# One run instead of two for the small products at the start of the recurrence

## The chip, the cores and the metric

One core of one Trainium2 chip runs the whole program. The metric is device time in microseconds of one execution, taken as the median over several; the time before is 921.15 us (three runs, 920.98 to 921.52). The engines are named as the profile names them: PE does matrix products (PEld its weight loads), DVE, ACT and POOL do elementwise work, SP issues transfers.

## The reference, cut to what matters

Two layers. In each, a normalised input of 512 tokens by 1024 features is projected, and the projection feeds two branches: 16 heads of sliding-window attention, and 8 heads of a gated linear recurrence. The gated outputs are projected back, normalised and added. The recurrence is what the change touches:

```
def step(state, xs):                       # one chunk, all heads
    qch, kch, vch, b = xs                  # b: running sum of log forget gates
    decay = where(causal, exp(b_t - b_s), 0)
    scores = einsum('bhtd,bhsd,bhtsd->bhts', qch, kch, decay)
    o = einsum('bhts,bhsv->bhtv', scores, vch)
    o = o + einsum('bhtd,bhdv->bhtv', qch * exp(b), state)
    state = exp(b_last) * state + einsum('bhsd,bhsv->bhdv', kch * exp(b_last - b), vch)
```

## The kernel before, in words

Projections are done in `step()` (line 293): one step issues three products of 128x512, because every float32 operand is split in a high and a low half (`whi`, `wlo` for weights, made by ACT line 181 and DVE line 182; `hhi`, `hlo`, `ops` for the other operand). A *unit* is one output tile of a projection; it gathers in one of three PSUM banks named `pj`, and an evacuation on ACT or DVE (lines 851, 865, 889, 893) frees the bank. Up to two units run in turns.

The recurrence is worked out per head from small to large blocks. For each head, `prepare` makes `kb` and `qb`; `spread` (line 694) forms the base blocks of two tokens as 16 products of 32x32 outputs; `keep_spread` (line 698) copies the wanted elements on DVE into the head's score tile `a`. Then `hgrn(a)` works on four heads at once and runs six levels, hh = 2, 4, 8, 16, 32, 64: products of `k` and `q` (line 750 for the first four levels, 756 and 761 for the last two) into PSUM banks `sc`, a scaling of `q` on DVE (768) and of `k` on POOL (769) that the next level's products need, and a masked copy of the products into `a` (778, or ACT lines 783 and 788). After that the states and outputs follow (lines 796 to 831). For heads 0, 1 and 4, 5 the base blocks are made at the end of `prepare`; for heads 2, 3 and 6, 7 they are made at the head of `hgrn`, into banks `ac`. The change is there.

What sets the order is `merge`: it takes turns between the recurrence generator and the stream of projection steps. Each `yield w` in the recurrence says how many units of its own total it has used, and the stream with the smaller share used goes next. The total of a recurrence pass is `HG_N` plus what `prepare` yields. So the sum of all yields in `hgrn` and `HG_N` belong together:

```
merge((chain(prepare(2), hgrn(0), prepare(4)), HG_N + 14), rest(("in", l, FQ + 3)))
merge((chain(prepare(6), hgrn(4)), HG_N + 7), rest(("out", l, "h0")))
```

PE products are pinned in program order. DVE, ACT and POOL instructions are placed by a scheduler, each engine then works its list strictly in order. hgrn(0) runs beside projections whose banks ACT frees; hgrn(4) runs beside output projections too, whose banks DVE frees at line 893.

Of the kernel before, what the change touches and what calls it, by code (L numbers as in the profile page):

```python
# [32 lines left out]

W_BUFS = 9
RAW_BUFS = 4
HG_N = 53.5
VLAG = 4
QWAIT = 8
ROT_WAIT = 8
# [31 lines left out]
def hybrid_kernel(ctx: ExitStack, tc: tile.TileContext, x, wkv, win, wout, g_pre, g_post, lbp, ghead, sinks,  # L71
# [26 lines left out]
    def ac():  # L98
        ac_turn[0] += 1
        return ac_tiles[ac_turn[0] % len(ac_tiles)]  # L100
# [30 lines left out]
    for l in range(1, DEPTH):  # L131
        i = plan_order.index((l, "kv"))
# [310 lines left out]
    def layer(l, last):  # L443
# [253 lines left out]
        def keep_spread(j, bank):  # L697
            nc.vector.copy_predicated(As[j].rearrange("p (n t) -> p n t", n=NT), bmask.unsqueeze(1).broadcast_to([P, NT, P]),
                                      bank.rearrange("p (n t) -> p n t", n=NT))
# [31 lines left out]
        def hgrn(a):  # L731
            hs = [(j, *quad.pop(a + j)) for j in range(4)]
            banks = [ac(), ac()]
            for i in range(2):
                spread(a + 2 + i, banks[i])
            for i in range(2):
                keep_spread(a + 2 + i, banks[i])
            yield 1.5
            for hh in (2, 4, 8, 16, 32, 64):
                nb = SEQ // (2 * hh)  # L740
                per, qu = nb // NT, nb // NT // 4
                Ls = [sc(), sc()]
                for j, f, k, q in hs:
                    L, i = Ls[j // 2], j % 2
                    qv = q.rearrange("p (b two j) -> p b two j", two=2, j=hh)
                    if hh <= 16:
                        for n in range(NT):
                            for b in range(4):
                                o_, blk, c = n * P + 32 * b, n * per + b * qu, 256 * i + n * 64 + 16 * b
                                pin(nc.tensor.matmul(L[32 * b:32 * b + 32, c:c + 16], lhsT=k[:, o_:o_ + 32],  # L750
                                                     rhs=qv[:, blk:blk + qu, 1, :], start=True, stop=True, tile_position=(0, 32 * b)))
                    elif hh == 32:
                        for n in range(NT):
                            for b in range(2):
                                o_, r_, c = n * P + 64 * b, 64 * b + 32 * (n % 2), 64 * i + n // 2 * 32
                                pin(nc.tensor.matmul(L[r_:r_ + 32, c:c + 32], lhsT=k[:, o_:o_ + 32],  # L756
                                                     rhs=q[:, o_ + 32:o_ + 64], start=True, stop=True, tile_position=(0, r_)))
                    else:
                        for n in range(NT):
                            o_, b, c = n * P, n % 2, 128 * i + n // 2 * 64  # L760
                            pin(nc.tensor.matmul(L[64 * b:64 * b + 64, c:c + 64], lhsT=k[:, o_:o_ + 64],
                                                 rhs=q[:, o_ + 64:o_ + 128], start=True, stop=True))
                for two in (hs[:2], hs[2:]):
                    for j, f, k, q in two:
                        qv = q.rearrange("p (b two j) -> p b two j", two=2, j=hh)
                        kv_ = k.rearrange("p (b two j) -> p b two j", two=2, j=hh)
                        tv = tots[a + j].rearrange("p (b two) -> p b two", two=2)
                        nc.vector.tensor_tensor(qv[:, :, 1, :], qv[:, :, 1, :], tv[:, :, 0].unsqueeze(2).broadcast_to([P, nb, hh]), op=ALU.mult)  # L768
                        nc.gpsimd.tensor_tensor(kv_[:, :, 0, :], kv_[:, :, 0, :], tv[:, :, 1].unsqueeze(2).broadcast_to([P, nb, hh]), op=ALU.mult)  # L769
                        t2 = sm.tile([P, nb], F32, tag=f"tot{hh}", name=f"tot{hh}", bufs=4)  # L770
                        nc.vector.tensor_tensor(t2, tv[:, :, 0], tv[:, :, 1], op=ALU.mult)
                        tots[a + j] = t2
                    for j, f, k, q in two:
                        A, L, i = As[a + j], Ls[j // 2], j % 2
                        if hh <= 16:
                            Av = A.rearrange("p (n b two j) -> p n b two j", n=NT, two=2, j=hh)[:, :, :, 1, :]
                            mv = lmask[hh].rearrange("p (b j) -> p b j", j=hh).unsqueeze(1).broadcast_to([P, NT, per, hh])
                            nc.vector.copy_predicated(Av, mv, L[:, 256 * i:256 * i + 256].rearrange("p (n b j) -> p n b j", n=NT, j=hh))
                        elif hh == 32:
                            Av = A.rearrange("p (m two t) -> p m two t", m=NT // 2, two=2)  # L780
                            for b in range(2):
                                for e in range(2):
                                    nc.scalar.copy(Av[64 * b:64 * b + 32, :, e, 64 * b + 32:64 * b + 64],
                                                   L[64 * b + 32 * e:64 * b + 32 * e + 32, 64 * i:64 * i + 64].rearrange("p (m t) -> p m t", m=NT // 2))
                        else:
                            Av = A.rearrange("p (m b t) -> p m b t", m=NT // 2, b=2)
                            for b in range(2):
                                nc.scalar.copy(Av[0:64, :, b, 64:128],
                                               L[64 * b:64 * b + 64, 128 * i:128 * i + 128].rearrange("p (m t) -> p m t", m=NT // 2))
                    yield 3.0  # L790

            kps = []
            for j, f, k, q in hs:
                KP = sc()
                for n in range(NT - 1):
                    pin(nc.tensor.transpose(KP[:, n * P:(n + 1) * P], k[:, n * P:(n + 1) * P], ident))  # L796
                kst_ = tmp("u") if j == 0 else tmp("s")
                nc.scalar.copy(kst_[:, 0:384], KP[:, 0:384])
                kps.append(kst_)
                if j % 2:  # L800
                    yield 1.0
            vs = lambda j, n: vt[a // 4, n][:, j * P:(j + 1) * P]
            sts = {}

            def states(j):
                SU = ac()
                for n in range(NT - 1):
                    pin(nc.tensor.matmul(SU[:, n * P:(n + 1) * P], lhsT=kps[j][:, n * P:(n + 1) * P], rhs=vs(j, n), start=True, stop=True))  # L808
                st = sm.tile([P, 3, P], F32, tag="st", name="st", bufs=2)
                nc.scalar.copy(st[:, 0], SU[:, 0:P])  # L810
                for n in range(1, NT - 1):
                    nc.vector.scalar_tensor_tensor(st[:, n], st[:, n - 1], tots[a + j][:, n:n + 1], SU[:, n * P:(n + 1) * P],
                                                   op0=ALU.mult, op1=ALU.add)
                sts[j] = st

            def outputs(j):
                q, A = hs[j][3], As[a + j]
                O = ac()
                for n in range(NT):
                    c = slice(n * P, (n + 1) * P)  # L820
                    pin(nc.tensor.matmul(O[:, c], lhsT=A[:, c], rhs=vs(j, n), start=(n == 0), stop=False))  # L821
                for n in range(1, NT):
                    c = slice(n * P, (n + 1) * P)
                    pin(nc.tensor.matmul(O[:, c], lhsT=q[:, c], rhs=sts[j][:, n - 1], start=False, stop=(n == NT - 1)))  # L824
                Ov = O.rearrange("p (n t) -> p n t", n=NT)
                sq = tmp("s")
                nc.scalar.activation(sq, O, AF.Square)
                ss = sm.tile([P, 4], F32, tag="hss", name="hss")
                nc.vector.tensor_reduce(ss, sq.rearrange("p (n t) -> p n t", n=NT), axis=AX.X, op=ALU.add)
                r = rstd_of(ss, 4, P, "hr")  # L830
                nc.vector.tensor_tensor(q.rearrange("p (n t) -> p n t", n=NT), Ov, r.unsqueeze(2).broadcast_to([P, NT, P]), op=ALU.mult)
                on[a + j] = q

            for fn, j, w in ((states, 0, 1.5), (states, 1, 1.5), (outputs, 0, 2.0), (states, 2, 1.5), (outputs, 1, 2.0),
                             (states, 3, 1.5), (outputs, 2, 2.0), (outputs, 3, 2.0)):
                fn(j)
                yield w
# [342 lines left out]
```

## Time and profile before

| | |
|---|---|
| median of the runs | 921.15 us (920.98 to 921.52) |
| profiled execution, its own time | 922.98 us |
| its span, first to last instruction | 921.3 us |
| mean granted TensorE clock | 0.998 |
| PE busy | 904.2 us, 98% of the span |
| DVE, ACT, POOL busy | 667.0, 463.8, 273.9 us |
| HBM traffic | 108 GB/s over the span |

The span is the first to the last instruction on the core; 1.68 us of the execution's own time lie around it. A busy PE is read with care, since products overlap: a product of 128x512 is booked with 0.39 us, but they start 0.227 us apart. So starts are compared here, not durations. Rows of the timeline have the start, the time from the first start to the last end, the engine, the line, what is written from what, the shape and the count.

### The profile page before, as it was taken

The page shows a single profiled execution, that of the slowest core. Times are in us where ns is not written, and L with a number is a line of the kernel's source. Part 1 is how long each engine was busy: PE and PEld are TensorE (multiplying, and loading weights), DVE is VectorE, ACT ScalarE, POOL GpSimd, SP SyncE. Part 2 cuts the span into 40 slices and gives each one's busy share as a digit, 9 for nine tenths or more (in the row PEclk, how much of TensorE's full clock was granted, in tenths as well). Part 3 has the DMA queues.
Part 4 walks back from the last instruction along what each step waited for, and adds up shares of the span by engine and source line. Part 5 has one row for each costly group of instructions (what it writes and reads, how often), then busy time and mean ns, then how long its engine had stood idle before and what let it go on. Part 6 is the DMA issues. An engine that isn't in the chain of part 4 may idle for free.

```text
span 921.3 us, 19004 instructions
## 1 busy us (share of the span) xinstructions
PE 904.2 (98%) x7240; PEld 752.5 (82%) x7240; DVE 667.0 (72%) x1326; ACT 463.8 (50%) x1100; POOL 273.9 (30%) x292
## 2 busy tenths in 40 slices
PE   8999999999999999999999999999999999999996
PEld 6888887888888888888888878888888888888885
DVE  4977878859854797655786689776889449866556
ACT  5535757653664423534563466686446463245242
POOL 3424444303413042121332254451144022330102
PEclk9999999999999999999999999999999999999999
DMA  7594613322222332333355656122322323213413
GB/s 224 153 259 130 172 43 92 92 81 85 91 69 70 107 103 82 92 95 119 131 168 167 168 141 179 57 70 92 94 70 81 99 73 94 82 47 93 137 35 137
DMA packets 56570, 100.74 MB, mean 109 GB/s; under 512 B 6560, under 2 KB 9120, under 8 KB 56480
## 3 DMA queue, kind: packets, MB, share of 16 engines
q1 hardware_dynamic: 56192, 99.40, 36.4%
q8 instruction: 57, 0.93, 0.4%
q14 instruction: 33, 0.27, 0.1%
q10 hardware_dynamic: 288, 0.14, 0.1%
HBM read 86.93 MB, written 12.58 MB: 108 GB/s over the span
## 4 chain that ended last, share of the span: by engine, by line
PE 89%; DVE 6%; ACT 2%; issue 1%; POOL 1%; DMA 0%; POOLq 0%; DVEq 0%; ACTq 0%
PE pj L293 73%; PE sc L567 2%; PE ac L620 2%; PE sc L750 2%; PE ac L821 2%; DVE wlo L182 1%; PE ac L824 1%; PE ac L808 1%; PE sc L594 1%; ACT s L581 1%; PE sc L873 1%; PE sc L406 1%; PE sc L796 1%; DVE a L954 0%; PE sc L556 0%
## 5 line engine op out<-in xcount | busy, mean ns | idle before, releaser
L182 DVE TENSOR_TENSOR wlo<-raw,whi 128x512 fp32r<-128x512 f32 x249 | 182.8, 748 | 49.5 <-ACT whi L181 48.8
L181 ACT CAST whi<-raw 128x512 fp32r<-128x512 f32 x256 | 154.1, 620 | 105.9 <-PE pj L293 95.1
L293 PE MATMUL pj<-hhi,wlo 128*128 128x512 f32 x512 | 203.8, 398 | 0.0
L293 PE MATMUL pj<-hhi,whi 128*128 128x512 f32 x512 | 199.8, 390 | 0.0
L293 PE MATMUL pj<-hlo,whi 128*128 128x512 f32 x512 | 199.5, 390 | 0.0
L293 PE MATMUL pj<-whi,ops 128*128 128x512 f32 (+1 forms) x520 | 172.5, 394 | 0.0
L293 PEld LDWEIGHTS pj<-whi,ops 128*128 128x128 f32 x520 | 97.3, 188 | 19.3
L293 PEld LDWEIGHTS pj<-hhi,whi 128*128 128x128 f32 x512 | 96.1, 188 | 20.7
L293 PEld LDWEIGHTS pj<-hhi,wlo 128*128 128x128 f32 x512 | 96.2, 188 | 19.3
L293 PEld LDWEIGHTS pj<-hlo,whi 128*128 128x128 f32 x512 | 96.2, 188 | 18.6
L293 PE MATMUL pj<-whi,hlo 128*128 128x512 f32 x256 | 103.6, 405 | 0.0
L293 PE MATMUL pj<-wlo,ops 128*128 128x512 f32 (+1 forms) x260 | 100.8, 388 | 0.0
L293 PE MATMUL pj<-wlo,hhi 128*128 128x512 f32 x256 | 100.4, 392 | 0.3 <-DVE wlo L182 0.2
L293 PE MATMUL pj<-whi,hhi 128*128 128x512 f32 x256 | 100.3, 392 | 0.0
L769 POOL TENSOR_TENSOR k<-k,tot 128x256 f32<-128x256 f32 x80 | 64.6, 835 | 106.0 <-PE sc L750 56.5
L581 ACT ACTIVATE s<-sc,negm 128x128 f32<-128x128 f32 x128 | 45.5, 368 | 38.5 <-DVE negm L575 38.5
L768 DVE TENSOR_TENSOR q<-q,tot 128x256 f32<-128x256 f32 x80 | 48.3, 641 | 12.8 <-PE sc L756 7.0
L293 PEld LDWEIGHTS pj<-whi,hhi 128*128 128x128 f32 x256 | 48.1, 188 | 10.3
L293 PEld LDWEIGHTS pj<-wlo,ops 128*128 128x128 f32 x260 | 49.0, 188 | 8.8
L293 PEld LDWEIGHTS pj<-wlo,hhi 128*128 128x128 f32 x256 | 48.3, 189 | 8.8 <-DVE wlo L182 1.0
L293 PEld LDWEIGHTS pj<-whi,hlo 128*128 128x128 f32 x256 | 48.2, 188 | 8.1
L588 POOL TENSOR_TENSOR s<-s,sums 128x512 f32<-128x512 f32 x32 | 34.1, 1066 | 44.2 <-DVE sums L586 29.2
(188 smaller groups left out, 1418.1 us busy)
## 6 DMA issues: line engine op xcount, KB each, us to landing
raw<-in_win_dram SPq DMA_DIRECT2D x192, 256.0 KB, 2.7
raw<-in_wout_dram SPq DMA_DIRECT2D x64, 256.0 KB, 2.7
stack<-rot SPq DMA_DIRECT2D x16, 512.0 KB, 3.4
qs<-stack SPq DMA_DIRECT2D x32, 256.0 KB, 4.7
a<-in_x_dram SPq DMA_DIRECT2D x12, 256.0 KB, 3.7
raw<-in_wkv_dram SPq DMA_DIRECT2D x8, 256.0 KB, 4.1
x_mid<-a SPq DMA_DIRECT2D x8, 256.0 KB, 2.6
a<-x_mid SPq DMA_DIRECT2D x8, 256.0 KB, 3.2
```

The costliest lines, as they stand in the source:

```text
L181: keep(nc.scalar.copy(hi, v))
L182: keep((nc.gpsimd if i in on_pool and i % 2 else nc.vector).tensor_tensor(lo, v, hi.bitcast(F32), op=ALU.subtract))
L293: nc.tensor.matmul(u.o, lhsT=u.sta(k, u.w)[i], rhs=u.mov(k, u.w)[j], start=(n == 0), stop=(n == len(u.list) - 1))
L406: pin(nc.tensor.transpose(o[:, j * P:(j + 1) * P], self.xn[:, c, j * P:(j + 1) * P], ident))
L567: pin(nc.tensor.matmul(S[:, h * 256:(h + 1) * 256], lhsT=q[:, 2 * hp_ + h, t_], rhs=kst[v][p][:, (n - 1) * P:(n + 1) * P], start=(h == 0 a ...
L581: nc.scalar.activation(pt[:, h * P:(h + 1) * P], cur[h], AF.Exp, bias=negm[:, h:h + 1], scale=SCALE, accum_out=sums[:, h:h + 1])
L588: nc.gpsimd.tensor_tensor(pv, pv, sums.unsqueeze(2).broadcast_to([P, 4, P]), op=ALU.mult)
L620: pin(nc.tensor.matmul(U, lhsT=vst[v][:, blk, :], rhs=d, start=(i == 0), stop=(i == len(terms) - 1)))
L750: pin(nc.tensor.matmul(L[32 * b:32 * b + 32, c:c + 16], lhsT=k[:, o_:o_ + 32], rhs=qv[:, blk:blk + qu, 1, :], start=True, stop=True, tile_ ...
L768: nc.vector.tensor_tensor(qv[:, :, 1, :], qv[:, :, 1, :], tv[:, :, 0].unsqueeze(2).broadcast_to([P, nb, hh]), op=ALU.mult)
L769: nc.gpsimd.tensor_tensor(kv_[:, :, 0, :], kv_[:, :, 0, :], tv[:, :, 1].unsqueeze(2).broadcast_to([P, nb, hh]), op=ALU.mult)
L821: pin(nc.tensor.matmul(O[:, c], lhsT=A[:, c], rhs=vs(j, n), start=(n == 0), stop=False))
```

## The change

At the head of `hgrn`, the base blocks of the third and fourth head move from before the first pause to behind it, so that on PE they stand straight ahead of the products of level hh = 2. The pause is now 3.5 units and stands ahead of both (it was 1.5 and stood between them). The copies `keep_spread` are now issued behind the products of that first level. `HG_N` grows by the same two units.

```diff
-HG_N = 53.5
+HG_N = 55.5
...
         def hgrn(a):
             hs = [(j, *quad.pop(a + j)) for j in range(4)]
             banks = [ac(), ac()]
+            yield 3.5
             for i in range(2):
                 spread(a + 2 + i, banks[i])
-            for i in range(2):
-                keep_spread(a + 2 + i, banks[i])
-            yield 1.5
             for hh in (2, 4, 8, 16, 32, 64):
...
+                for i in range(2 if hh == 2 else 0):
+                    keep_spread(a + 2 + i, banks[i])
                 for two in (hs[:2], hs[2:]):
```

PE in hgrn(0) of the first layer, before: L293 are projection products, L694 the base blocks (each row 16 products into one bank), L750 the first level.

```order
L694 MATMUL ac_82<-b 32x32 x16
L694 MATMUL ac_81<-b 32x32 x16
L293 MATMUL pj<-hhi,wlo 128x512
L293 MATMUL pj<-hlo,whi 128x512
L293 MATMUL pj<-hhi,whi 128x512
L293 MATMUL pj<-hhi,wlo 128x512
L293 MATMUL pj<-hlo,whi 128x512
L293 MATMUL pj<-hhi,whi 128x512
L293 MATMUL pj<-hhi,wlo 128x512
L293 MATMUL pj<-hlo,whi 128x512
L293 MATMUL pj<-hhi,whi 128x512
L750 MATMUL sc_78<-q,k 32x16 x32
```

The same place after (the level's products are now line 748):

```order
L293 MATMUL pj<-hhi,wlo 128x512
L293 MATMUL pj<-hlo,whi 128x512
L293 MATMUL pj<-hhi,whi 128x512
L694 MATMUL ac_82<-b 32x32 x16
L694 MATMUL ac_81<-b 32x32 x16
L748 MATMUL sc_78<-q,k 32x16 x32
L748 MATMUL sc_79<-q,k 32x16 x32
L293 MATMUL pj<-hhi,wlo 128x512
```

Nine projection products stood between the two groups, none does now; the joint group stands 18 projection products later than the base blocks did and nine later than the first level did. The same holds in all four passes (two per layer). From there the levels stand 9 to 3 projection products later than before, and from the second pair of transposes (line 796) on where they did.

DVE in hgrn(4) of the first layer, from the base blocks' copies (L698) through level hh = 4, before. L852 and L854 belong to the attention gate, L182 to weights, L893 frees two `pj` banks.

```order
L182 TENSOR_TENSOR wlo<-raw,whi 128x512
L768 TENSOR_TENSOR q<-q,tot_3809 128x64x4
L854 TENSOR_TENSOR ops<-z_3885,ops 128x512
L768 TENSOR_TENSOR q<-q,tot_3813 128x64x4
L778 COPY_PREDICATED a<-masks,sc_80 128x64x4 x2
L768 TENSOR_TENSOR q<-q,tot_3855 128x64x4
L768 TENSOR_TENSOR q<-q,tot_3859 128x64x4
L778 COPY_PREDICATED a<-masks,sc_78 128x64x4 x2
L893 TENSOR_TENSOR y<-pj,y 128x512 x2
```

And after:

```order
L182 TENSOR_TENSOR wlo<-raw,whi 128x512
L854 TENSOR_TENSOR ops<-z_3885,ops 128x512
L768 TENSOR_TENSOR q<-q,tot_3824 128x64x4
L768 TENSOR_TENSOR q<-q,tot_3828 128x64x4
L778 COPY_PREDICATED a<-masks,sc_80 128x64x4 x2
L768 TENSOR_TENSOR q<-q,tot_3870 128x64x4
L768 TENSOR_TENSOR q<-q,tot_3874 128x64x4
L778 COPY_PREDICATED a<-masks,sc_78 128x64x4 x2
L893 TENSOR_TENSOR y<-pj,y 128x512 x2
```

L854 has left the level's chain; the two evacuations L893 still stand behind all of the level's own work.

PE in hgrn(4), where the transposes of a gate (L873) and those of the recurrence (L796) are, before:

```order
L796 MATMUL sc_80<-ident,k 128x128 x3
L796 MATMUL sc_78<-ident,k 128x128 x3
L293 MATMUL pj<-whi,ops 128x512
L293 MATMUL pj<-wlo,ops 128x512
L293 MATMUL pj<-whi,ops 128x512
L873 MATMUL sc_79<-ident,z_4574 128x128 x4
L293 MATMUL pj<-whi,hlo 128x512
L293 MATMUL pj<-wlo,hhi 128x512
L293 MATMUL pj<-whi,hhi 128x512
L293 MATMUL pj<-whi,ops 128x512
L293 MATMUL pj<-wlo,ops 128x512
L293 MATMUL pj<-whi,ops 128x512
```

After:

```order
L873 MATMUL sc_80<-ident,z_4574 128x128 x4
L796 MATMUL sc_78<-ident,k 128x128 x3
L796 MATMUL sc_79<-ident,k 128x128 x3
L293 MATMUL pj<-whi,hlo 128x512
L293 MATMUL pj<-wlo,hhi 128x512
L293 MATMUL pj<-whi,hhi 128x512
L293 MATMUL pj<-whi,ops 128x512
L293 MATMUL pj<-wlo,ops 128x512
L293 MATMUL pj<-whi,ops 128x512
L796 MATMUL sc_80<-ident,k 128x128 x3
```

They stand in one run now, and the gate's transposes are in bank sc_80, which the second pair of L796 takes six projection products later. Before, that pair stood next behind the rows shown, and bank sc_80 came to it from the first pair.

## The prediction

> **What bounds the kernel.** I read the page first (busy shares, the granted clock, the chain), then what PE waits for, then the timeline around the places that the change moves.
>
> ```profile
> PE 904.2 (98%) x7240; PEld 752.5 (82%) x7240; DVE 667.0 (72%) x1326; ACT 463.8 (50%) x1100; POOL 273.9 (30%) x292
> ...
> PEclk9999999999999999999999999999999999999999
> ...
> PE 89%; DVE 6%; ACT 2%; issue 1%; POOL 1%; DMA 0%; POOLq 0%; DVEq 0%; ACTq 0%
> ```
>
> PE is busy 98% of the span at full granted clock, and 89% of the chain that ended last is PE's own work. The answer on PE's waits leaves nothing to win in the recurrence: its longest entry is
>
> ```profile
> PE sc L567 <- ACT s L581: 2.7, 5, 0.8
> ```
>
> and L567 is attention. So a change there counts in two ways alone: by the PE time that the instructions themselves take, and by waits that it makes where there was none. First the PE time, in hgrn(0) of the first layer:
>
> ```profile
> 204.69 0.39 PE L293 MATMUL pj<-hhi,whi 128*128 128x512 f32 x1
> ...
> 209.45 0.39 PE L293 MATMUL pj<-hhi,whi 128*128 128x512 f32 x1
> 209.77 0.76 PE L694 MATMUL ac<-b 128*32 128x32 f32 x64
> 210.46 0.50 PE L293 MATMUL pj<-hhi,wlo 128*128 128x512 f32 x1
> 210.80 0.40 PE L293 MATMUL pj<-hlo,whi 128*128 128x512 f32 x1
> ...
> 212.42 0.40 PE L293 MATMUL pj<-hhi,whi 128*128 128x512 f32 x1
> 212.75 1.34 PE L750 MATMUL sc<-q,k 128*32 128x16 f32 x128
> 214.01 0.50 PE L293 MATMUL pj<-hhi,wlo 128*128 128x512 f32 x1
> 214.35 0.40 PE L293 MATMUL pj<-hlo,whi 128*128 128x512 f32 x1
> ...
> 221.72 1.41 PE L750 MATMUL sc<-q,k 128*32 128x16 f32 x128
> ```
>
> The reader is to compare starts. From 204.69 to 209.45 there are 21 projection products: 4.76/21 = 0.2267 us each. Around the base blocks, 209.45 to 210.80 is 1.35 us for two such steps (0.453), so the run of 64 costs 0.90 us. (A product written in the code is two in the trace: 32 and 64 are booked as 64 and 128.) The run of the first level, 212.42 to 214.35, costs 1.93 - 0.453 = 1.48 us for 128. The 64 more cost 0.58 us, 9.1 ns each, so 0.90 - 0.58 = 0.32 us of a run does not hang on its length: the first small product starts 0.32 instead of 0.227 us after the last large one, the first large one comes 0.12 us behind the small ones and its successor 0.34 us later.
>
> **The change part by part.**
>
> *Two runs become one.* Before: 0.90 + 1.48 = 2.38 us. After: 0.32 + 192 x 9.1 ns = 2.07 us. Saved 0.31 to 0.32 us. The products behind a run go a little slowly too: 210.80 to 212.42 is 1.62 us for seven steps that make 1.59 at full pace; that 0.03 falls away once. Together 0.35 us a place. How many places there are:
>
> ```profile
> L694 PE MATMUL ac<-b x256: 196/196/217, 209.8 to 772.1; 128*32 128x32 f32 x128
> ```
>
> 256 = four runs of 64, two passes in two layers. So 4 x 0.35 = 1.40 us. A run of 192 is not in the trace. Bounds from the nearest rows: two level runs of the same 128 products last 1.34 and 1.41 us, so waits inside a run move it by some 0.07 us; with as much again for a longer run, 0.35 +- 0.11 a place, 1.0 to 1.8 us in all. I take the middle, since the first level's own row (1.34) is the one that is joined.
>
> *Transposes.* In hgrn(4) the order puts L873 and the first pair of L796 into one run. Their rows before, first layer:
>
> ```profile
> 381.46 0.39 PE L293 MATMUL pj<-whi,hhi 128*128 128x512 f32 x1
> 381.69 0.82 PE L796 MATMUL sc<-ident,k 128*128 128x128 f32 x6
> ...
> 382.58 0.40 PE L293 MATMUL pj<-wlo,ops 128*128 128x512 f32 x1
> 382.81 0.40 PE L293 MATMUL pj<-whi,ops 128*128 128x512 f32 x1
> 383.05 0.60 PE L873 MATMUL sc<-ident,z 128*128 128x128 f32 x4
> ...
> 383.72 0.39 PE L293 MATMUL pj<-wlo,hhi 128*128 128x512 f32 x1
> ...
> 384.87 0.38 PE L796 MATMUL sc<-ident,k 128*128 128x128 f32 x2
> ```
>
> By the same reckoning six cost 0.67 us (381.46 to 382.58 less 0.453) and four 0.46, so 0.105 a product and 0.04 a run: wide products have hardly any price of switching. Two layers, 0.07 us.
>
> *The pauses and HG_N.* Both grow by two units; they issue nothing. The number of all other PE products stays. Sum: 1.40 + 0.07 = 1.47 us off PE, all on the path, as PE waits for nothing there. The profiled span 921.3 would become 919.8, with the 1.68 us around it a time of 921.5 for an execution that took 922.98. The median of the runs is 921.15, so I forecast 921.15 - 1.47 = 919.7 us.
>
> *What must stay hidden: the copies of the base blocks (L698).* They now stand on DVE between the joint run and the first level's scalings. DVE and POOL of hgrn(0) before:
>
> ```profile
> 210.61 1.35 DVE L698 COPY_PREDICATED a<-masks,ac 128x512 f32<-128x512 uint8 x2
> ...
> 213.27 0.43 DVE L768 TENSOR_TENSOR q<-q,f 128x256 f32<-128x256 f32 x1 [0.37 <-PE sc L750]
> ...
> 218.56 0.75 DVE L768 TENSOR_TENSOR q<-q,f 128x256 f32<-128x256 f32 x2
> ```
>
> The last scaling ended at 219.31, the next level began at 221.72 in the quoted row: 2.4 us to spare. After: with the joint run's start as zero, the copies can begin at 0.84 (as 210.61 follows 209.77) and end at 2.2. Then two L768, two L778, two L768; before, that stretch took 6.0 us (213.27 to 219.31) with gate and weight work in it that now comes later. Even with all of it the scalings end at 8.2. The next level starts 33 projection products behind the joint run: 2.07 + 33 x 0.227 = 9.6. At least 1.4 us to spare. What DVE cannot do while L698 waits for PE is only weights and gate work that the new order puts behind; PE has not one wait of note on them above.
>
> *The evacuations of the output projection in hgrn(4) (L893).* Here the level hh = 4 moves nine projection products later while the projection units keep their place, and L893 stands behind the level's work on DVE. The rows before, PE's first:
>
> ```profile
> 331.88 1.34 PE L750 MATMUL sc<-q,k 128*32 128x16 f32 x128
> ...
> 339.87 0.62 PE L293 MATMUL pj<-whi,ops 128*128 128x512 f32 x2
> ```
>
> ```profile
> 333.99 0.89 DVE L768 TENSOR_TENSOR q<-q,tot 128x256 f32<-128x256 f32 x1
> 334.81 1.16 DVE L854 TENSOR_TENSOR ops<-z,ops 128x512 fp32r<-128x512 f32 x1
> 335.89 0.89 DVE L768 TENSOR_TENSOR q<-q,tot 128x256 f32<-128x256 f32 x1
> 336.70 0.75 DVE L778 COPY_PREDICATED a<-masks,sc 128x256 f32<-128x256 uint8 x2
> ...
> 338.69 1.28 DVE L893 TENSOR_TENSOR y<-pj,y 128x512 f32<-128x512 f32 x2
> ```
>
> By the order, the second product of the row at 339.87 (start 340.10) opens a unit in the bank that the first L893 frees (end 338.69 + 0.64 = 339.33): 0.77 us to spare, the tightest place of the pass. After, that product starts at 340.10 - 0.35 = 339.75. The level starts at 331.88 + 9 x 0.227 - 0.35 = 333.57; its first scaling can start some 0.52 us later (213.27 behind 212.75) at 334.1. L854 (1.16) now stands ahead of the chain; without it 333.99 to 338.69 is 4.70 - 1.08 = 3.62 us, so the chain ends at 337.7 and L893's first at 338.4. Some 1.4 us to spare, 0.3 if the chain were as long as before. I cost it at nothing.
>
> *The bank of the transposes.* L796's second pair now needs the bank of L873 six projection products later:
>
> ```profile
> 383.68 0.69 ACT L875 ACTIVATE ops<-sc,gh 128x512 fp32r<-128x512 f32 x1 [0.41 <-PE sc L873]
> ```
>
> ```profile
> 384.41 0.75 DVE L876 SCALAR_TENSOR_TENSOR ops<-sc,gh,ops 128x512 fp32r<-128x512 f32 x1 [1.17 <-ACT ops L875]
> ```
>
> L873 started at 383.05, L876 ended at 385.16: 2.1 us. After, PE has 0.46 + 0.67 + 6 x 0.227 = 2.5 us. 0.4 us to spare, if no weight work (0.62 on ACT) slips ahead.
>
> **The rivals.**
>
> *The joint run saves more.* If it also loses the waits inside a first-level run and the slow pace behind it, the upper bound of 0.46 a place holds: 1.84 + 0.07 = 1.9 us, 919.2. For it: level runs differ by 0.07 among themselves. Against: the first level's row is already the shorter one.
>
> *A new wait takes it back.* Both tight banks above in both layers: L893 late by 0.3 (the margin used up and DVE beside POOL as slow as before), L873's by 0.3 to 0.7. 2 x 0.8 = 1.6 us, 921.2 or no change. For it: margins of 0.3 to 1.4 us. Against: by the orders the work that made the chain long has moved out of it.
>
> *PE's instructions run dry, and the kernel is slower.* The code comes in by its own queue:
>
> ```profile
> q8 instruction: 57, 0.93, 0.4%
> ```
>
> ```profile
> L694 PEld LDWEIGHTS ac<-b x256: 106/109/113, 209.8 to 772.1; 128*32 128x32 f32 x128
> ```
>
> Product and load come in pairs (7240 of each on the page), 14480 instructions in 57 packets: 254 a packet. A packet takes 0.4% x 16 x 921.3/57 = 1.03 us (0.9 to 1.2 with the rounding). The longest run so far has 256 instructions, about one packet, used up in 1.16 us; the joint run has 384, one and a half. If the next packet but one is asked for only when a packet is used up, each joint run stands still for up to 1.03 us: 4 x 1.03 = 4.1, and 919.7 + 4.1 = 923.8 us. It decides from 0.36 us a place, where the gain is gone; above 0.83 us the kernel is slower by over 0.2%. Against: 128-product runs pass at the same 9.1 ns from start to end, though many must cross a packet's border. [...]
>
> **How the numbers follow.** Forecast 0.62, more saved 0.18, a new wait 0.13, code running dry 0.07. The likeliest gives 919.7. The low end is a little below the upper bound of the saving (919.2), 918.9; the high end takes in the case of new waits, 921.4. A measurement of this kernel tells a change of about 0.2% (1.84 us, so 919.31 or less) from none. The case of more saving lies below that for the most part, and a tenth or so of the forecast's own range: faster 0.25. Slower needs code running dry in nearly full size: 0.06. The rest, 0.69, is within 0.2%.
>
> **What would show it.** In the trace after: four runs of L694 and L748 together whose cost by starts is 2.0 to 2.2 us; no gap in them beyond 0.15 us (a gap near 1 us would be the code); no new entry for L293, L748 or L796 among PE's waits; PE's busy time and the span shorter by about the same 1.5 us. I am wrong if the joint run costs as much as the two did, or if PE waits for L893, L876 or L768.

## The result, and the profile after

The kernel after takes 927.88 us (median of 5 runs, 926.09 to 928.45) against 921.00 us of the kernel before on the same chip; the ratio is 1.0069, with a 95% interval of [1.0058, 1.0081]. It is slower by 6.9 us. The profiled execution took 927.92 us with a span of 926.2 us. The page of the kernel after, then the answer on PE's waits:

```profile
PE 904.2 (98%) x7240; PEld 753.2 (81%) x7240; DVE 665.4 (72%) x1326; ACT 464.2 (50%) x1100; POOL 267.9 (29%) x292
...
q8 instruction: 57, 0.93, 0.4%
...
PE 87%; DVE 6%; ACT 3%; issue 2%; POOL 1%; DMA 0%; DVEq 0%; POOLq 0%; ACTq 0%
```

```profile
PE sc L748 <- issue: 5.4, 2, 3.1
PE sc L567 <- ACT s L581: 3.5, 6, 0.8
```

PE's busy time is the same to 0.1 us, and "issue" has gone from 1% to 2% of the chain. The new first entry of the waits is the first level's products (L748): PE stood still twice, 5.4 us in all, for nothing that a semaphore shows. The timeline of PE at the first joint run:

```profile
212.46 0.39 PE L293 MATMUL pj<-hhi,whi 128*128 128x512 f32 x1
212.78 0.75 PE L694 MATMUL ac<-b 128*32 128x32 f32 x63
...
213.35 1.36 PE L748 MATMUL sc<-q,k 128*32 128x16 f32 x127
214.64 0.50 PE L293 MATMUL pj<-hhi,wlo 128*128 128x512 f32 x1
214.98 0.40 PE L293 MATMUL pj<-hlo,whi 128*128 128x512 f32 x1
```

From 212.46 to 214.98 less two steps (0.453) is 2.07 us, the figure of the prediction. The fourth place costs 2.07 as well. The second place:

```profile
321.33 0.39 PE L293 MATMUL pj<-hhi,whi 128*128 128x512 f32 x1
321.65 0.75 PE L694 MATMUL ac<-b 128*32 128x32 f32 x63
...
322.23 1.16 PE L748 MATMUL sc<-q,k 128*32 128x16 f32 x98
325.68 0.44 PE L748 MATMUL sc<-q,k 128*32 128x16 f32 x29 [2.30 <-issue]
326.05 0.50 PE L293 MATMUL pj<-hhi,wlo 128*128 128x512 f32 x1
326.38 0.39 PE L293 MATMUL pj<-hlo,whi 128*128 128x512 f32 x1
...
327.19 0.63 PE L293 MATMUL pj<-hlo,whi 128*128 128x512 f32 x1
327.62 0.63 PE L293 MATMUL pj<-hhi,whi 128*128 128x512 f32 x1
...
330.18 0.47 PE L293 MATMUL pj<-hhi,whi 128*128 128x512 f32 x1
...
330.71 0.39 PE L293 MATMUL pj<-hlo,whi 128*128 128x512 f32 x1
```

Here the run breaks off after 98 + 1 of the level's 128 products. By starts it costs 326.38 - 321.33 - 0.453 = 4.60 us. The gap has a sequel: from 327.19 to 330.18 seven products start 0.43 us apart instead of 0.227. The view by windows gives the granted clock of that stretch in its third column from the right:

```profile
318.00:321.00 3.00, 3.00 (x15) 2.49 (x14) 2.04 (x5) 2.15 (x4) 0.00 (x0) 1.00 0.01 2
326.92:330.34 3.42, 3.42 (x10) 2.65 (x9) 1.19 (x3) 0.77 (x2) 0.54 (x1) 0.50 0.27 91
```

It was 1.00 before the run and 0.50 for 3.4 us behind it. From 326.38 to 330.71 twelve steps take 4.33 us, which make 2.72 at full pace: 1.6 us more. The third place has a longer gap, and full pace behind it:

```profile
668.15 0.39 PE L293 MATMUL pj<-hhi,whi 128*128 128x512 f32 x1
668.47 0.75 PE L694 MATMUL ac<-b 128*32 128x32 f32 x63
...
669.05 1.18 PE L748 MATMUL sc<-q,k 128*32 128x16 f32 x105
673.37 0.38 PE L748 MATMUL sc<-q,k 128*32 128x16 f32 x22 [3.14 <-issue]
673.67 0.50 PE L293 MATMUL pj<-hhi,wlo 128*128 128x512 f32 x1
674.01 0.39 PE L293 MATMUL pj<-hlo,whi 128*128 128x512 f32 x1
```

674.01 - 668.15 - 0.453 = 5.41 us. The sum: (4.60 - 2.07) + 1.6 + (5.41 - 2.07) = 7.5 us lost, 1.47 saved as forecast, so +6.0 us. Another 0.8 is attention's wait on L581, 2.7 us before and 3.5 now; what is added stands at 89.5 us, ahead of the first place that the change moves. That makes 6.8 us. The two traces differ by less, 926.2 - 921.3 = 4.9 us, because the execution traced before got off later: its first projection product starts at 10.06 us, that of the kernel after at 8.20, and 6.8 - 1.9 = 4.9. So the sum accounts for the two traces. That it also comes near the 6.9 us between the medians says less, since a start that varies by 1.9 us stands in those too.

**Where the gaps stand.** Count PE's recorded instructions by their starts (loads, products, semaphore instructions, drains). The two gaps follow the 5057th and the 9921st, 4864 = 19 x 256 apart. So both sit on the same grid of 256, with the remainder 193; a place of this grid is called a border here. The instruction queue brings 0.93 MB in 57 packets, 16 KB each, and the 14692 recorded instructions hold just 57 such borders. In the second place its transfers stand like this; the answer on DMA for the window 323.2 to 324.2 us has

```profile
q8 instruction: 1, 0.02, 5.7%
```

and the windows on both sides of it, 321.9 to 323.2 and 324.2 to 327.4, have none. On the grid, the joint run at the second place meets a first border after its 72nd instruction (at 321.96 us) and the next one 256 further on, where the gap is. The packet is fetched from 323.22 to 324.14, and PE goes on at 325.68, 3.7 us after the first border and 1.5 us after the packet has landed. At the third place: first border after 85 instructions (668.84), packet from 670.92 to 671.88, PE on at 673.37, 4.5 us. The joint runs at the first and fourth place meet their first border after 236 and 177 of 384 instructions, and the next one lies outside.

**Theory A** (the author's, drawn from these two gaps, where PE passes the first border without a stop and stands still at the second): PE has two blocks of 256 instructions at hand. Only when it has passed a border is a new block asked for, and that block is usable 3.7 to 4.5 us later, the times at these two places. A run of small products uses up a block in 1.16 us (128 products at 9.1 ns), so a run that holds two borders runs dry at the second. **Rival B:** the gap belongs to the place or to the joining itself: a wait for data, for a bank or for a queue that the profile does not name. **Rival C:** the moved order costs something in all places.

### The profile page after: what moved, and what is told of

Its sections match the earlier page's. It is cut to its first block, busy times and chain, and to the rows that moved or that the text cites. A ratio compares the mean times of both kernels' runs of the same rounds, so it can differ in the third digit from the quotient of the medians.

```text
span 926.2 us, 18994 instructions
## 1 busy us (share of the span) xinstructions
PE 904.2 (98%) x7240; PEld 753.2 (81%) x7240; DVE 665.4 (72%) x1326; ACT 464.2 (50%) x1100; POOL 267.9 (29%) x292
## 4 chain that ended last, share of the span: by engine, by line
PE 87%; DVE 6%; ACT 3%; issue 2%; POOL 1%; DMA 0%; DVEq 0%; POOLq 0%; ACTq 0%
PE pj L293 72%; PE sc L748 2%; PE sc L567 2%; PE ac L620 2%; PE ac L821 2%; ACT s L581 1%; DVE wlo L182 1%; PE ac L824 1%; PE ac L808 1%; PE sc L594 1%; PE sc L873 1%; PE sc L796 1%; DVE a L340 1%; PE sc L406 1%; DVE a L954 0%
## 5 line engine op out<-in xcount | busy, mean ns | idle before, releaser
L182 DVE TENSOR_TENSOR wlo<-raw,whi 128x512 fp32r<-128x512 f32 x249 | 179.5, 737 | 49.5 <-ACT whi L181 48.0
L293 PE MATMUL pj<-hhi,wlo 128*128 128x512 f32 x512 | 203.7, 398 | 0.0
L293 PE MATMUL pj<-hlo,whi 128*128 128x512 f32 x512 | 200.2, 391 | 0.0
L293 PE MATMUL pj<-hhi,whi 128*128 128x512 f32 x512 | 200.2, 391 | 0.0
L293 PE MATMUL pj<-whi,ops 128*128 128x512 f32 (+1 forms) x520 | 172.5, 394 | 0.0
L293 PEld LDWEIGHTS pj<-hhi,whi 128*128 128x128 f32 x512 | 96.5, 189 | 20.7
L293 PEld LDWEIGHTS pj<-whi,ops 128*128 128x128 f32 x520 | 97.3, 188 | 19.3
L293 PEld LDWEIGHTS pj<-hhi,wlo 128*128 128x128 f32 x512 | 96.5, 189 | 19.4
L293 PEld LDWEIGHTS pj<-hlo,whi 128*128 128x128 f32 x512 | 96.6, 189 | 18.9
L293 PE MATMUL pj<-whi,hlo 128*128 128x512 f32 x256 | 103.6, 405 | 0.0
L293 PE MATMUL pj<-wlo,ops 128*128 128x512 f32 (+1 forms) x260 | 100.7, 387 | 0.0
L293 PE MATMUL pj<-wlo,hhi 128*128 128x512 f32 x256 | 100.4, 392 | 0.3 <-DVE wlo L182 0.2
L293 PE MATMUL pj<-whi,hhi 128*128 128x512 f32 x256 | 100.3, 392 | 0.0
L769 POOL TENSOR_TENSOR k<-k,tot 128x256 f32<-128x256 f32 x80 | 61.1, 791 | 120.1 <-PE sc L748 74.4
L581 ACT ACTIVATE s<-sc,negm 128x128 f32<-128x128 f32 x128 | 45.6, 369 | 39.5 <-DVE negm L575 39.4
L768 DVE TENSOR_TENSOR q<-q,tot 128x256 f32<-128x256 f32 x80 | 54.0, 715 | 15.4 <-PE sc L748 10.8
L293 PEld LDWEIGHTS pj<-whi,hhi 128*128 128x128 f32 x256 | 48.1, 188 | 10.3
L293 PEld LDWEIGHTS pj<-wlo,ops 128*128 128x128 f32 x260 | 49.0, 188 | 8.8
L293 PEld LDWEIGHTS pj<-wlo,hhi 128*128 128x128 f32 x256 | 48.3, 189 | 8.9 <-DVE wlo L182 1.0
L293 PEld LDWEIGHTS pj<-whi,hlo 128*128 128x128 f32 x256 | 48.2, 188 | 8.1
```

What stands on the lines that cost most here:

```text
L182: keep((nc.gpsimd if i in on_pool and i % 2 else nc.vector).tensor_tensor(lo, v, hi.bitcast(F32), op=ALU.subtract))
L293: nc.tensor.matmul(u.o, lhsT=u.sta(k, u.w)[i], rhs=u.mov(k, u.w)[j], start=(n == 0), stop=(n == len(u.list) - 1))
L581: nc.scalar.activation(pt[:, h * P:(h + 1) * P], cur[h], AF.Exp, bias=negm[:, h:h + 1], scale=SCALE, accum_out=sums[:, h:h + 1])
```

## The experiments

In the table, "joint at" names the places where the two groups are one run, and "first borders" says how many PE instructions of each of these runs come before its first border. The ratio goes by the executions of the kernel before that ran beside each version: their medians are 921.00 us for the kernel after, 921.27 for e1 to e4, 921.78 for e5 to e8 and 920.98 for e9.

| run | joint at | first borders | time, us | ratio to before |
|---|---|---|---|---|
| after | all | 236, 72, 85, 177 | 927.88 | 1.0069 [1.0058, 1.0081] |
| e1_pad128 | all | 108, 200, 213, 49 | 929.05 | 1.0088 [1.0071, 1.0105] |
| e2_pad64 | all | 172, 8, 21, 113 | 924.95 | 1.0039 [1.0024, 1.0054] |
| e3_outer | 1, 4 | 236, 177 | 920.78 | 0.9996 [0.9987, 1.0005] |
| e4_inner | 2, 3 | 73, 86 | 927.77 | 1.0080 [1.0055, 1.0104] |
| e5_step | none | see below | 924.56 | 1.0030 [1.0019, 1.0041] |
| e6_phased | all | 172, 8, 174, 10 | 921.31 | 0.9995 [0.9986, 1.0004] |
| e7_three | 1, 2, 3 | 172, 8, 21 | 920.53 | 0.9989 [0.9980, 0.9998] |
| e8_before_pads | none | - | 923.57 | 1.0021 [1.0013, 1.0030] |
| e9_rotating | all | 164, 0, 182, 18 | 920.00 | 0.9987 [0.9978, 0.9996] |

**e1_pad128: the whole program moved by half a block.**

```diff
     pin(nc.tensor.matmul(warm, lhsT=ones[:, 0:P], rhs=ones, start=True, stop=True))
+    for k in range(32):
+        pin(nc.tensor.matmul(warm[0:32, 0:32], lhsT=ones[:, 0:32], rhs=ones[:, 0:32], start=True, stop=True,
+                             tile_position=(0, 0)))
     for k in range(KT):
```

> The kernel after, with 32 more small products at the program's start, where PE waits for its first data anyway (128 recorded PE instructions: 64 weight loads and 64 products, into a bank that is overwritten). Nothing else moves; every later PE instruction has a place 128 higher. Theory A (PE's code comes in blocks of 256 instructions, and a joint run of 384 that holds two borders of blocks runs dry at the second): first border in the four joint runs, counted from the run's start, before 236, 72, 85, 177, now 108, 200, 213, 49. So the gaps leave the second and third place (2.07 us by starts there) and stand in the first and the fourth, 2.3 to 3.2 us each; the time stays within 925.5 to 928.5. Rival B (the gap belongs to the place: a wait for data, for a bank or for a queue that the profile does not name): gaps of 2.3 and 3.1 us stay at the second and third place, none at the first and fourth, 927.9. Should the pad itself lie on the path, it costs up to 0.6 us under both.

The timeline of PE, first and fourth place (the first rows of each run left out), and between them the third:

```profile
214.24 1.28 PE L748 MATMUL sc<-q,k 128*32 128x16 f32 x116
218.59 0.30 PE L748 MATMUL sc<-q,k 128*32 128x16 f32 x11 [3.07 <-issue]
...
670.84 1.39 PE L748 MATMUL sc<-q,k 128*32 128x16 f32 x127
...
779.69 0.98 PE L748 MATMUL sc<-q,k 128*32 128x16 f32 x87
782.99 0.57 PE L748 MATMUL sc<-q,k 128*32 128x16 f32 x40 [2.32 <-issue]
```

The gaps have moved to the first and fourth place. By starts the four runs cost 5.62, 2.07, 2.10 and 4.58 us, and 1.35 us of half pace follows the first. Places that ran freely before now stand still, with the same data, banks and queues. Rival B is out. The time is 0.5 us above the range; it also holds the added products, whose price was not measured here.

**e2_pad64: a quarter of a block.** The same edit with `range(16)`.

> As the run with 128 more instructions, with 16 products (64 instructions). Theory A: first borders at 172, 8, 21, 113. No gap at the first place; the full gap, 2.3 to 3.2 us, at the fourth, where two borders lie in the run; at the second and third the first border comes so early in the run that its fetch may have been asked for while the large products still ran, so 0 to 1.5 us each. Time 921.5 to 925.5, so less than the kernel after by 2.4 us or more. Rival B: gaps at the second and third place as in the kernel after, 927.9.

PE at the second, third and fourth place:

```profile
321.23 1.36 PE L748 MATMUL sc<-q,k 128*32 128x16 f32 x127
...
663.78 1.46 PE L748 MATMUL sc<-q,k 128*32 128x16 f32 x127
...
772.80 1.29 PE L748 MATMUL sc<-q,k 128*32 128x16 f32 x119
777.32 0.31 PE L748 MATMUL sc<-q,k 128*32 128x16 f32 x8 [3.23 <-issue]
```

One gap is left, where A has it (5.79 us by starts, and 2.5 of half pace behind it). The second and third run hold two borders each, at 8 and 264, 21 and 277, and pass: 2.07 and 2.17 us. Their packets start at 317.41 and 661.21, which is 3.3 and 2.1 us before the borders are executed. The kernel after has the same among large products: at 22 of its 26 borders in L293 the packet starts 0.3 to 4.3 us ahead of the border (at 205.86 for the border at 210.19). So here a border early in a run counts as passed before the run. That is a detail which A left open between 0 and 1.5 us; it is near 0 up to the 21st instruction.

**e3_outer and e4_inner: the join at two places only.**

```diff
-            yield 3.5
+            joint = (l, a) in ((0, 0), (1, 4))          # e4_inner: ((0, 4), (1, 0))
+            if joint:
+                yield 3.5
             for i in range(2):
                 spread(a + 2 + i, banks[i])
+            if not joint:
+                for i in range(2):
+                    keep_spread(a + 2 + i, banks[i])
+                yield 1.5
...
-                for i in range(2 if hh == 2 else 0):
+                for i in range(2 if hh == 2 and joint else 0):
```

The passes that are not joint have 2 units less in their total, as before.

> The joint run only at the first and fourth place (layer 0 hgrn(0), layer 1 hgrn(4)); the other two as in the kernel before. Theory A: no place has two borders in a run (236 and 177), no gap, two places of 0.35 us saved: 920.3 (919.9 to 920.8). Rival C (the loss is a cost of the moved order that all places share, as later copies, later evacuations or a lower clock): half of the loss, 924.4.

> The converse: the joint run only at the second and third place (layer 0 hgrn(4), layer 1 hgrn(0)); the other two as in the kernel before. Theory A: first borders at 73 and 86, both gaps stay, and the saving of the two good places is gone: 928.6 (927 to 929.5). Rival C: half of the loss, 924.4.

The outer places cost 2.07 us each without a gap, and the kernel takes 0.49 us less than before, of 0.70 expected; the interval of the ratio takes in no change too. The inner ones alone have the whole loss. PE's waits of the inner version:

```profile
PE sc L754 <- issue: 5.4, 2, 3.2
```

Its runs cost 4.49 and 5.43 us; this time it is the third place that half pace follows (1.6 us), not the second. Rival C, half of the loss in each, is out.

**e5_step: three large products between the two groups.**

```diff
-            yield 3.5
+            yield 3.0
             for i in range(2):
                 spread(a + 2 + i, banks[i])
+            yield 0.5
```

> The order of the kernel after, but with one projection step (three large products) between the base blocks and the first level in all four places, so no run is longer than 257 instructions and nothing is joined. Theory A (two blocks of 256 instructions held, a new one asked for about 1.3 us after a border and usable some 3.7 to 4.6 us after it): at the second and third place a border lies in the base blocks (instruction 78 and 92 of them) and the next one in the level run (its instruction 200 and 213), some 2.1 to 2.3 us later, so gaps of 1.4 to 2.5 us stand there, exactly at these instructions; none at the first and fourth place. 924 to 927 us. Rival B (it is the joint run itself: 192 small products without a large one between them overrun something): no gap, nothing saved, 921.2. Nine large products between, as in the kernel before, have no gap under either.

PE at the second and the third place:

```profile
322.44 1.10 PE L749 MATMUL sc<-q,k 128*32 128x16 f32 x99
325.56 0.44 PE L749 MATMUL sc<-q,k 128*32 128x16 f32 x29 [2.02 <-issue]
...
669.89 0.38 PE L749 MATMUL sc<-q,k 128*32 128x16 f32 x22 [0.96 <-issue]
```

Nothing is joined and the gaps are there, after 99 and 106 of the 128 products (instructions 198 and 212, forecast 200 and 213). They are 2.02 and 0.96 us, the second shorter than forecast: its packet starts 0.9 us after the border, not 1.3. So it is not the joining that costs: with three large products the two borders stand 2.2 us apart, too little time. Nine of them are only just enough. In the kernel before, the same two borders stand 3.5 us apart (662.70 and 666.21 at the third place) and PE passes. In e3_outer the third place has the order of the kernel before, and PE stands still a little at the second border, 1.2 us after a packet that landed at 662.38:

```profile
662.19 1.22 PE L754 MATMUL sc<-q,k 128*32 128x16 f32 x114
663.63 0.31 PE L754 MATMUL sc<-q,k 128*32 128x16 f32 x14 [0.21 <-issue]
```

**e6_phased and e8_before_pads: the borders moved out of all four runs, and the price of doing so.** To the kernel after (e6) and the kernel before (e8), 16 products are added at the start as above, and 26 in the second layer's normalisation:

```diff
             o = sc()
+            for k in range(26 if self.hT is hT.get(1) and self.tt == 2 and c == 0 else 0):
+                pin(nc.tensor.matmul(o[0:32, 0:32], lhsT=ident[:, 0:32], rhs=ident[:, 0:32], start=True, stop=True,
+                                     tile_position=(0, 0)))
             for j in range(4):
```

> The kernel after with 16 more small products at the program's start and 26 more in the second layer's first normalisation (ahead of transposes that wait 0.55 us for DVE), which put the first borders of the four joint runs at 172, 8, 174 and 10. Theory A: at 172 and 174 only one border lies in the run, at 8 and 10 the first is passed so early that its fetch was asked for during the large products; no gap anywhere, 2.07 us by starts at all four places. 921.2 - 1.47 + 0 to 0.6 for the added products = 919.7 to 920.4. Rival B: gaps at second and third place, 927 to 928.

> The kernel before with the same 16 and 26 added products: their own price. All theories: no gap in a run of small products (the longest has 259 instructions); both groups stand where PE waits for something else, so 921.2 to 921.8.

No joint run of e6 has a gap. The four cost 2.07, 2.17, 2.07 and 2.07 us, so A holds. In e8, against the expectation, the level run of the second place lasts 1.57 us instead of 1.34; it stands still for 0.25 us at a border 3.5 us behind another. Both times missed their ranges, e6 by 0.9 us and e8 by 1.8. The ranges went by 921.2 us for the kernel before, which took 921.78 beside them; the rest shows that the added products are not free: e8 is 1.8 us slower than the kernel before. The timeline of PE shows the second group in e8:

```profile
465.89 1.83 PE L406 MATMUL sc<-ident 128*32 128x32 f32 x52
```

52 products take 1.83 us; without the last one's own 0.196 that is 32 ns each and not the 9.1 of the recurrence. The recurrence's products change from tile to tile of 32 columns; these all use the same one. Against its own base e8, joining is worth 923.57 - 921.31 = 2.3 us; by the one trace of each, 0.8 of it is again attention's wait on ACT (3.5 us in e8, 2.7 in e6), and the other 1.5 has the size of the forecast saving.

**e7_three: no second group, the fourth place split.** `joint = (l, a) != (1, 4)` and 16 products at the start.

> 16 more small products at the program's start, the joint run at the first three places, the fourth as in the kernel before. Theory A: first borders at 172, 8 and 21; no gap over 0.1 us, three savings of 0.35 us less 0.1 at the third place, and 0 to 0.3 us for the added products: 920.2 to 920.6. Rival B: gaps at the second and third place, 927 to 928.

No gap in the joint runs, which cost 2.07, 2.07 and 2.17 us; the kernel is 1.25 us below the kernel before. In the fourth place, which is split, a border falls right behind the level's run, and the second large product there starts 0.58 us after the first instead of 0.34.

**e9_rotating: all four, with cheaper products.**

```diff
-            for k in range(26 if self.hT is hT.get(1) and self.tt == 2 and c == 0 else 0):
-                pin(nc.tensor.matmul(o[0:32, 0:32], lhsT=ident[:, 0:32], rhs=ident[:, 0:32], start=True, stop=True,
-                                     tile_position=(0, 0)))
+            for k in range(22 if self.hT is hT.get(1) and self.tt == 2 and c == 0 else 0):
+                pin(nc.tensor.matmul(o[32 * (k % 4):32 * (k % 4) + 32, 0:32], lhsT=ident[:, 0:32], rhs=ident[:, 0:32],
+                                     start=True, stop=True, tile_position=(0, 32 * (k % 4))))
...
-    for k in range(16):
+    for k in range(18):
```

The 18 products at the start turn through the tiles of their bank in the same way.

> The joint run in all four places, with 18 and 22 added products at the same two points as in the run with 16 and 26, but turning through the four 32-row tiles as the recurrence's own small products do, instead of all into one tile: the 52 product instructions of one tile took 1.83 us there, 35 ns each, against 9.1 ns for the turning ones. First borders at 164, 0, 182 and 18. Theory A: no gap in any joint run; the added products cost 44 x 9.1 ns = 0.4 us ahead of the transposes, which wait 0.55 us there anyway, and about 0.4 to 0.8 us at the start, so 919.9 to 920.6 against 921.2 to 921.8 of the kernel before. Rival B: gaps at the second and third place, 927 to 928.

PE's waits, its second group of added products, and the joint run at the third place:

```profile
PE sc L569 <- ACT s L583: 2.7, 5, 0.8
PE sc L408 <- DVE hlo L416: 1.6, 2, 1.3
```

```profile
464.02 0.60 PE L406 MATMUL sc<-ident 128*32 128x32 f32 x44
...
663.85 0.75 PE L696 MATMUL ac<-b 128*32 128x32 f32 x63
...
664.42 1.36 PE L750 MATMUL sc<-q,k 128*32 128x16 f32 x127
```

No entry for the joint runs is left among the waits. All four cost 2.07 us, and the 44 added products (0.60 - 0.196)/43 = 9.4 ns each. It has the lowest time, 920.00 against 920.98 us of the kernel before, 0.9987 [0.9978, 0.9996]; by the ratios e7_three, with 0.9989 [0.9980, 0.9998], is as good.

## Why the prediction was wrong

*Two runs become one: right.* The term of 0.35 us a place, with a run of 2.07 us, is what every run without a gap cost: 2.07 to 2.17 us in all 20 of them.

*Transposes: right.* The joined run in hgrn(4), PE's timeline of the kernel after:

```profile
384.27 0.39 PE L293 MATMUL pj<-whi,ops 128*128 128x512 f32 x1
384.50 0.60 PE L873 MATMUL sc<-ident,z 128*128 128x128 f32 x4
384.94 0.82 PE L796 MATMUL sc<-ident,k 128*128 128x128 f32 x6
385.51 0.48 PE L293 MATMUL pj<-whi,hlo 128*128 128x512 f32 x1
385.83 0.40 PE L293 MATMUL pj<-wlo,hhi 128*128 128x512 f32 x1
```

385.83 - 384.27 - 0.453 = 1.11 us, against 0.67 + 0.46 apart: 0.02 to 0.03 saved here, 0.07 forecast for both layers.

*The covers: right.* No wait of PE for L768, L893 or L876 has come up. DVE's tight evacuations behind the second place, in the kernel after and in e9 (two lines further down in its source):

```profile
340.62 1.28 DVE L893 TENSOR_TENSOR y<-pj,y 128x512 f32<-128x512 f32 x2
...
335.83 1.28 DVE L895 TENSOR_TENSOR y<-pj,y 128x512 f32<-128x512 f32 x2
```

No product waits for the banks that they free, and e9, with the join in all four places, has no loss either. The margin was smaller than forecast: in e9, where no gap delays PE, the first evacuation ends at 335.83 + 0.64 = 336.47 and the product that the prediction names starts at 336.94. That leaves 0.5 us, nearer to the 0.3 of an unshortened chain than to the 1.4.

*The failed step: "PE's instructions run dry".* The sum of the forecast put this at nothing ("all on the path, as PE waits for nothing there"), and that is what failed: PE waited for its code in two of the four joined runs, and the gaps with the half pace behind one of them cost 7.5 us. As a rival the mechanism was named, with the right sign. Its chance (0.07) and its price were wrong in three ways.

- Depth. How much code PE has at hand the step only supposed, and it argued against itself with "128-product runs pass at the same 9.1 ns from start to end, though many must cross a packet's border". One border inside cost nothing, that is true (2.07 us for the runs of e3_outer, with first borders at 236 and 177), and it says nothing of two. A run of 256 instructions has two borders at most at its very ends; 384 instructions can hold two well inside. The length against the packet, which the step had worked out as one and a half, was the argument to weigh. The gap stands at the second border in all nine cases (seven joint runs and the two places of e5). That fits the two blocks of Theory A; the depth itself no trace shows.
- Size. 1.03 us was the time of a packet's transfer. What counts is the time from the first border to PE going on. In the seven joint runs with a gap the packet starts 1.3 to 2.2 us after the border, takes 0.9 to 1.9, and PE goes on 1.3 to 1.5 us after it has landed: 3.6 to 4.6 us, of which the run itself covers some 1.2. That leaves 2.4 to 3.4 us a gap. Half pace came on top behind four of the seven (1.35 to 2.5 us).
- Number. Four places were assumed. It is two, chosen by where the grid of 256 falls, which neither the diff nor the order of the instructions tells until the instructions are counted, and where the grid starts (193) was read off the gaps themselves.

*The range.* Its high end, 921.4, took in a new wait on data; one on code, with its 7.5 us 927, was left out with the 0.07.

## What to carry to other kernels

Before small products are packed into one run, count instructions (load and product each one) and not only microseconds: here 384 in a row stood still for 2.4 to 3.4 us wherever two borders of 256 fell between their 49th and 369th instruction. Two shorter runs with three large products between them counted together (e5). What decided was the time between two borders that small products reach: at 1.2 us the gaps were 2.4 to 3.4 us, at 2.2 us (e5) 1.0 and 2.0, and at 3.5 us, the order of the kernel before, there was none in that kernel, 0.21 us in e3_outer and 0.25 in e8_before_pads. Such a loss hangs on the position in the whole program, so an edit ahead of it, here of 64 instructions that do nothing (e2_pad64), moves it or takes it away; when a harmless edit costs some microseconds and PE waits for "issue", look at the count. Where a wait is argued away with a row that crosses one border, ask what the new run does that no row has done.

## What the runs showed of the hardware that was not expected

- The nine gaps all stand at the remainder 193 of a grid of 256 instructions, and the traces have 57 packets of 16 KB (kernels before and after) or 58 (e9_rotating), just as many as there are borders in their 14692 to 14859 recorded instructions. From this the author takes it that PE's code comes in blocks of 256 instructions. In the joint runs with a gap PE went on 3.6 to 4.6 us after the border before that one, always 1.3 to 1.5 us after the packet had landed. What sets the 0.9 to 2.2 us from a border to the start of the packet was not looked for. By the measured starts PE needs a block in 1.16 us in a small run (9.1 ns for two instructions) and in 29 us among large products (0.227 us for two).
- A border in the first 21 instructions of a run did no harm (2.07 to 2.17 us by starts in e2_pad64, e6_phased, e7_three and e9_rotating): there the packet started 2 to 4 us before the border was reached (3.3 and 2.1 in e2_pad64).
- After four of the seven gaps of 2.4 to 3.4 us large products start 0.43 us apart, with a granted clock of 0.50 for 3.4 us (6.8 in e2_pad64). It was not always the longer gap. The granted clock changes at 6.07, 326.92, 330.34 and 920.84 us in the trace of the kernel after, and at 10.54 and 918.48 in that of the kernel before; the distances, 320.85, 3.413, 590.51 and 907.95 us, are 94, 1, 173 and 266 times 3.413. Cut by this grid, PE's idle time at the second place of the kernel after lies with 2.17 us in one stretch of 3.413, and half pace follows; that at the third place, 3.14 us, falls into two stretches, 1.44 and 1.70, and full pace follows. By the grids of their own traces half pace also follows 3.07 us in one stretch in e1, 2.58 in e2 and 2.04 in e4, and none follows the other four gaps (e5's two among them), which have 1.7 us or less in any. No run was made to test this.
- Small products into one and the same tile of 32 columns started 32 ns apart (52 in e8_before_pads), those that turn through the four tiles 9.4 ns (44 in e9_rotating).
- Attention's wait on ACT was 2.7 or 2.8 us (5 times) in most versions and 3.5 us (6 times) in the kernel after and in e8_before_pads, with no edit there. In both the added wait stands at about 89 us, ahead of the moved places. Its cause was not looked for.
